# A decoder layer in fp32 on one Trainium2 core: the output projection's sums, subtractions and loads put at other places, and early heads' work stepped once per piece

## The chip, the cores and the metric

The kernel runs on one core of a Trainium2 chip. The core has five engines with a queue of instructions each: TensorE (PE in the profile, with its weight loads as PEld), VectorE (DVE), ScalarE (ACT), GpSimd (POOL) and SyncE (SP), which here issues the DMAs. An engine works its queue in order, and semaphores hold it until what it reads is there. The metric is the device time of one execution in microseconds (us), the median of several runs.

## The reference

The kernel computes one layer of a hybrid decoder on 512 tokens with 2048 features, in float32:

```python
h = rms_norm(x, norm1_w)
q, k, v, z, xbc, dt_raw = split(h @ w_in)     # 8 heads x 128; 16 SSD heads x 64
attn = moba_attention(rms_norm(q), rms_norm(k), v)          # causal, blocks of 256
ssm = grouped_rms_norm(ssd_chunked_scan(silu(conv4(xbc)), dt) * silu(z))
x = x + concat([attn, ssm]) @ w_out                         # out projection, 2048 x 2048
h = rms_norm(x, norm2_w)
u_gate, u_val = split(conv3(h @ w_up))                      # 2048 x (2 x 5632)
return x + (silu(u_gate) * u_val) @ w_down                  # 5632 x 2048
```

## The kernel before

Every float32 operand is split into a rounded high part and the rest (`hi` by ScalarE, `lo` = operand minus hi by VectorE), and a product is three matmuls: hi by hi, hi by lo, lo by hi.

**Stages.** From 0 to about 626 us runs the input projection. Its weights come in pieces (`pieces`), and between pieces TensorE does the small products of heads whose inputs are there: attention heads in pairs p = 0 to 3, two SSD groups. Each head's work is a Python generator (`g_q`, `g_head`, `g_ssm`, `g_pair`) that yields between steps; `spawn` starts it, and `advance` lets each waiting generator do one step if by the planner's clocks (`clk`) its input is ready. `advance` is called after each piece in the main loop and once in the middle of a piece (`fm_uses` at `kk == 2`, `tok_use` at half its order). A step's products write to `sm`, of which there are three PSUM buffers. A call of `advance` thus sets how many big products (`acc<-...`) stand between a projection's end and the step that needs its result.

Then come the three seven-product projections: out (626 to about 850 us), up (to 1660) and down (to 2130, three passes). A 2 x 2 block product is made from seven products instead of eight. Work is in **groups**: 8 for out (`m`, 0 to 7), 44 for up, 3 x 8 for down. A group has weight tiles of 128 x 1024 for its four quarters (`rawb` for "21" and "22", `rawa` for "11", "12" and "22b", `load`) and sums of them, the chain in `add`: s1 = 21 + 22, s2 = s1 − 11, s3 = 21 := 11 − 21, s4 = 12 − s. All are on VectorE but s3 (line 1044), which is on GpSimd. The chain's tile `s` lies in PSUM, but for group 0, where it is `acc_s` in SBUF. On the other side stand seven **kinds** (`cmb` tiles, KT1, K11, KT2, K21, KT3, K22, KT4): the activations' quarters and sums of them, split in high and low, used by all groups of a projection.

An **item** is one product of one group, 24 matmuls of 128 x 256 in the full case; a **slot** is the item's number. Items go P5, P3 of the group before, P1, P4 of the group before, P6, P2, P7. After each item `step_slot` issues, in this order: what stands in the table `events` for the slot, the low split of two items on (`split_lo(slot + 2)`), what stands in the table `after`, and the high split of three items on. So the order within VectorE's queue is the order of these calls; the tables are filled by `at(slot, fn, where=...)`.

**What the change touches in the out projection.** `acc(gi)` (line 1280) loads the two rows of x to which group m is added, tile `acc`, from `xT`. `down_after` (L1188) adds each finished product into it. When a row is done (P3 or P4), `out_row` scales it into `gx` (L1214, ScalarE), squares it into `sq`, adds that to `rbc` (L1212, VectorE), and on the second row makes the quarter sums of `gx` for the up projection (`sums`: L955 for 128 x 512, L957 and L958 for 128 x 256), and writes `gx` to `xd` in DRAM. For m = 7 the sums and the first two kinds of the up projection are made at once, without the trip through DRAM. `kinds_of` loads the other kinds' raw halves (`ld`, `lx`, `twin`) and splits them at given slots (`b_split`, L390 and L391, in `after`); `pairs_split` splits the part that comes from `gx`. KT2 and K21 of the out projection are loaded ready-made from `mk` (L1151).

Of the kernel before, what the change touches and what calls it, by code (L numbers as in the profile page):

```python
# [188 lines left out]
def body(ctx, tc, xT, wi, wz, wo, wu, wd0, wd1, wd2, pp, pf, outT, dbg={}):  # L189
# [151 lines left out]

    def spawn(g, urgent=False):
        step([g, 0.0, urgent, 0])

# [19 lines left out]

    def advance(force=False):

        for e in list(gens):
            e[3] += 1
            ready_ = clk["pe"] >= e[1]
            if force or (e[2] and (ready_ or e[3] > 1)) or \  # L370
                    (ready_ and max(clk["act"], clk["dve"]) < clk["pe"] + BEHIND):
                step(e)
# [106 lines left out]
    def g_ssm(g, sg):  # L479
# [101 lines left out]
        for i in range(2):  # L581
            spawn(g_pair(2 * g + i, ms[i]))

# [19 lines left out]
    def g_head(acc, hd):  # L603
# [26 lines left out]
        for half in range(2):  # L630
# [75 lines left out]
            if pr["n"] == 4:  # L706
                spawn(g_pair(4 + hd["i"] // 2, pr["m"]))

# [33 lines left out]
    def fm_uses(R, k0, nks, nk_tot, box, done):  # L742

        uses = []
        for nk in nks:
            def use(h, l, k0=k0, nk=nk):
                if k0 == 0:
                    box["acc"] = acc_tile()
                for kk in range(nk):
                    if kk == 2:  # L750
                        advance()
                    k = k0 + kk
                    rh, rl = R(k)
# [23 lines left out]
    def tok_use(k0, nk, cols, box, done):  # L777

        def use(h, l):
# [5 lines left out]
            for n, (kk, t) in enumerate(order):  # L785
                if n == len(order) // 2:
                    advance()
                k = k0 + kk
# [116 lines left out]
    def add_pair(p):  # L905
        pr = {}
        hds = [{"i": 2 * p + i, "pair": pr} for i in range(2)]
        q_, k_ = ([lambda acc, i=i, f=f: spawn(f(acc, hds[i])) for i in range(2)] for f in (g_q, g_head))
        for f in (q_[0], k_[0], q_[1]) if p < 3 else (k_[0], q_[0], k_[1], q_[1]):
# [27 lines left out]
    def z1_done(t, acc):  # L937
        A_.activation(sgs[1]["sz"][:, t, :], acc, AF.Silu, scale=rstd[:, t:t + 1])
        if t == 3:
            st["sz1"] = True  # L940
            spawn(g_ssm(1, sgs[1]))

# [80 lines left out]

    raw, chain, parts = {}, {}, {}
    cols = lambda gi: groups[gi]["n"] * 128
# [14 lines left out]
    def add(gi, name):  # L1040
        n = cols(gi)
        if name == "s3":
            r = raw[gi, "21"][:, :n]
            po.tensor_tensor(r, raw[gi, "11"][:, :n], r, op=OP.subtract)  # L1044
            return
# [25 lines left out]
    def split_lo(k):  # L1071
        if k >= len(items):
            return
        n = cols(items[k][0])
        h, src = parts[k]
# [4 lines left out]

    events, after = {}, {}

# [55 lines left out]
    def kinds_of(ph, base, todo, bufs, early, there=-99):  # L1138

        for k, ((t, q, n, src, slot), b) in enumerate(zip(todo, bufs)):  # L1140
            at(base + slot, b_split, ph, t, q, n, b, where=after)
            last = [j for j in range(k) if bufs[j] == b]
# [3 lines left out]

    for t, slot in ((KT2, -7), (K21, -4)):
        def whole(t=t):
# [5 lines left out]
    for t, slots in ((KT3, (1, 2)), (K22, (3, 4)), (KT4, (5, 6))):  # L1154
        todo += [(t, 4 * h, 4 - h, md[t][:, 4 * h:7 if h else 4], slots[h]) for h in range(2)]
    kinds_of("out", 0, todo, [0, 1, 2, 0, 1, 2], -2)
    for t, slot in ((KT2, 0), (K21, 1), (KT3, 2), (K22, 4), (KT4, 6)):
        at(slot, lambda t=t: pairs_split("out", t, 7, box["gx"][:, 1]), where=after)

# [5 lines left out]
    for t, slot in ((KT2, 9), (K21, 10), (KT3, 11), (K22, 13), (KT4, 15)):  # L1165
        at(base + slot, lambda t=t: pairs_split("up", t, 6, box["gx"]), where=after)
    for p in range(len(PASSES)):
# [33 lines left out]
    def out_row(g, r):  # L1201
# [5 lines left out]
        def square():  # L1207
            if m == 0 and r == 0:
                se.activation(rbc, a, AF.Square)
            else:  # L1210
                se.activation(box["sq"], a, AF.Square)
                ve.tensor_tensor(rbc, rbc, box["sq"], op=OP.add)  # L1212
# [3 lines left out]
        if m == 7:  # L1216
            if r:
                sums(ve, gx, 0)
                pairs_split("up", KT1, 6, box["gx"]), pairs_split("up", K11, 6, box["gx"])
                sums(ve, gx, 1)  # L1220
            square()
            return
        at(slot + 1, square, where=after)
        if r:
            at(slot + 1, sums, ve, gx, where=after)
            at(slot + 2, sy.dma_start, xd[:, m], gx)

# [52 lines left out]
    def acc(gi):  # L1280
        g = groups[gi]
        m, p = g["m"], g.get("p")
        if gi == D0:
            a = box["acc_s"].rearrange("p (a b) -> p a b", a=2)
        elif D0 < gi < D0 + 3:
# [154 lines left out]
```

## Time and profile before

| | |
|---|---|
| median of 3 runs (lowest, highest) | 2131.46 us (2129.65, 2133.74) |
| the profiled execution, its own time | 2131.46 us |
| its span | 2129.8 us |
| mean granted TensorE clock | 0.987 |
| TensorE busy | 2053.8 us, 96% |
| VectorE busy | 1675.9 us, 79% |
| ScalarE busy | 1014.9 us, 48% |
| GpSimd busy | 230.9 us, 11% |

The span goes from the first to the last instruction; the 1.7 us between it and the time lie around it. A busy time is that of instructions in work. An engine that stands in its queue on a semaphore isn't busy, and the profile names the instruction whose end released it. The granted clock is the share of full speed that TensorE got; 0.92 over 22 us means that 8% of them, 1.76 us, were lost. A row of the timeline gives start, length, engine, line, operation, tiles (written <- read) and shape, and in brackets the idle time before it and its releaser.

### The profile page before, as it was taken

The page shows a single profiled execution, that of the slowest core. Times are in us where ns is not written, and L with a number is a line of the kernel's source. Part 1 is how long each engine was busy: PE and PEld are TensorE (multiplying, and loading weights), DVE is VectorE, ACT ScalarE, POOL GpSimd, SP SyncE. Part 2 cuts the span into 40 slices and gives each one's busy share as a digit, 9 for nine tenths or more (in the row PEclk, how much of TensorE's full clock was granted, in tenths as well). Part 3 has the DMA queues.
Part 4 walks back from the last instruction along what each step waited for, and adds up shares of the span by engine and source line. Part 5 has one row for each costly group of instructions (what it writes and reads, how often), then busy time and mean ns, then how long its engine had stood idle before and what let it go on. Part 6 is the DMA issues. An engine that isn't in the chain of part 4 may idle for free.

```text
span 2129.8 us, 39110 instructions
## 1 busy us (share of the span) xinstructions
PE 2053.8 (96%) x15942; PEld 1961.0 (92%) x15942; DVE 1675.9 (79%) x2333; ACT 1014.9 (48%) x1428; POOL 230.9 (11%) x115
## 2 busy tenths in 40 slices
PE   9999999999998987999999999999999899999999
PEld 8888788888788987999999999999999899899999
DVE  6545555345568888999999999999999987977976
ACT  5433344343445345555555555555555643534533
POOL 0020000000001111011111111111111111111110
PEclk9999999999999999999999999999999999999999
DMA  5232233322256566354444544445446757757663
GB/s 193 74 108 86 70 122 97 98 93 85 80 203 232 186 236 216 131 188 156 161 164 164 187 152 164 163 167 184 154 160 211 236 200 260 253 204 267 221 197 124
DMA packets 126146, 353.96 MB, mean 166 GB/s; under 512 B 11728, under 2 KB 43664, under 8 KB 122256
## 3 DMA queue, kind: packets, MB, share of 16 engines
q1 hardware_dynamic: 125968, 351.48, 48.7%
q8 instruction: 125, 2.05, 0.4%
q14 instruction: 53, 0.43, 0.1%
HBM read 297.79 MB, written 53.64 MB: 165 GB/s over the span
## 4 chain that ended last, share of the span: by engine, by line
PE 82%; DVE 11%; DMA 2%; issue 2%; ACT 2%; SPq 0%; DVEq 0%; POOL 0%; ACTq 0%; POOLq 0%
PE x L1388 50%; PE acc L184 20%; PE y L1388 8%; PE sm L184 4%; DVE lo L1077 2%; DVE cmb L391 2%; DVE gx L955 1%; DMA acc<-xT 1%; DVE s L1051 1%; DVE acc L1188 1%; DVE s L1057 1%; DVE t L184 1%; ACT t L184 1%; ACT P L184 0%; DVE lo L184 0%
## 5 line engine op out<-in xcount | busy, mean ns | idle before, releaser
L1388 PE MATMUL x<-cmb,hi 128*128 128x256 f32 x6974 | 884.0, 279 | 30.8 <-DVE cmb L391 13.9
L1388 PEld LDWEIGHTS x<-cmb,hi 128*128 128x128 f32 x6974 | 837.5, 190 | 37.2 <-DVE cmb L391 17.3
L1388 PE MATMUL x<-cmb,lo 128*128 128x256 f32 x3422 | 465.9, 278 | 21.0 <-DVE lo L1077 16.0
L1388 PEld LDWEIGHTS x<-cmb,lo 128*128 128x128 f32 x3422 | 425.4, 189 | 22.8 <-DVE lo L1077 17.6
L1068 ACT ACTIVATE hi<-s 128x1024 fp32r<-128x1024 f32 (+1 forms) x225 | 225.5, 1002 | 352.8 <-DVE s L1051 215.0
L1044 POOL TENSOR_TENSOR rawb<-rawa,rawb 128x1024 f32<-128x1024 f32 (+1 forms) x76 | 192.8, 2537 | 1306.5 <-DVE s L1051 1278.6
L1077 DVE TENSOR_TENSOR lo<-s,hi 128x1024 fp32r<-128x1024 f32 (+1 forms) x225 | 267.2, 1188 | 18.9 <-issue 13.7
L1077 DVE TENSOR_TENSOR lo<-rawa,hi 128x1024 fp32r<-128x1024 f32 (+1 forms) x228 | 270.3, 1186 | 0.0
L1068 ACT ACTIVATE hi<-rawa 128x1024 fp32r<-128x1024 f32 (+1 forms) x228 | 234.3, 1031 | 42.5 <-PE x L1388 40.5
L184 DVE TENSOR_TENSOR lo<-raw,hi 128x512 fp32r<-128x512 f32 (+1 forms) x176 | 121.4, 691 | 152.3 <-ACT hi L184 150.8
L184 PE MATMUL acc<-A,hi 128*128 128x512 f32 x448 | 183.6, 410 | 0.7 <-ACT hi L184 0.7
L184 ACT ACTIVATE hi<-raw 128x512 fp32r<-128x512 f32 (+1 forms) x176 | 110.3, 627 | 147.4 <-PE acc L184 140.5
L184 PE MATMUL acc<-A,lo 128*128 128x512 f32 x448 | 177.8, 397 | 0.0
L184 PE MATMUL acc<-B,hi 128*128 128x512 f32 x448 | 177.7, 397 | 0.0
L1188 DVE TENSOR_TENSOR acc<-x,acc 128x256 f32<-128x256 f32 x174 | 73.3, 421 | 106.0 <-PE x L1388 99.8
L1388 PE MATMUL y<-cmb,hi 128*128 128x256 f32 x1184 | 148.0, 277 | 3.1 <-DVE cmb L391 3.1
L1233 ACT ACTIVATE cP<-x 128x256 f32<-128x256 f32 x132 | 50.7, 384 | 200.9 <-PE x L1388 200.9
L1388 PEld LDWEIGHTS y<-cmb,hi 128*128 128x128 f32 x1184 | 140.5, 188 | 3.7 <-DVE cmb L391 3.7
L184 PE MATMUL acc<-hi,A 128*128 128x256 f32 (+2 forms) x448 | 135.7, 303 | 0.0
L184 PE MATMUL acc<-hi,B 128*128 128x256 f32 (+2 forms) x448 | 133.9, 299 | 0.0
L184 PE MATMUL acc<-lo,A 128*128 128x256 f32 (+2 forms) x448 | 133.9, 299 | 0.0
L1068 ACT ACTIVATE hi<-rawb 128x1024 fp32r<-128x1024 f32 (+1 forms) x76 | 78.9, 1038 | 58.4 <-PE x L1388 31.8
(236 smaller groups left out, 2508.6 us busy)
## 6 DMA issues: line engine op xcount, KB each, us to landing
rawa<-wu SPq DMA_DIRECT2D x176, 512.0 KB, 3.8
raw<-wi SPq DMA_DIRECT2D x79, 512.0 KB, 3.7
rawa<-wd SPq DMA_DIRECT2D x64, 448.0 KB, 4.1
rawb<-wu SPq DMA_DIRECT2D x44, 512.0 KB, 4.7
gd<-gx SPq DMA_DIRECT2D x22, 1024.0 KB, 4.7
rawa<-wo SPq DMA_DIRECT2D x32, 512.0 KB, 4.8
rawa<-wd SPq DMA_DIRECT2D x32, 512.0 KB, 5.2
acc<-pd SPq DMA_DIRECT2D x16, 512.0 KB, 6.4
```

The source lines that it names most:

```text
L184: return fn(out, *args, **kw)
L391: vec.tensor_tensor(lo, src, hi.bitcast(F32), op=OP.subtract)
L955: E.tensor_tensor(g[:, 4:6, :], g[:, 1:4:2, :], g[:, 0:2, :], op=OP.subtract)
L1044: po.tensor_tensor(r, raw[gi, "11"][:, :n], r, op=OP.subtract)
L1051: ve.tensor_tensor(chain[gi][:, :n], raw[gi, "21"][:, :n], raw.pop((gi, "22"))[:, :n], op=OP.add)
L1057: ve.tensor_tensor(s_, raw[gi, "12"][:, :n], s_, op=OP.subtract)
L1068: se.activation(h[:, :n], src[:, :n], AF.Copy)
L1077: ve.tensor_tensor(l[:, :n], src[:, :n], h[:, :n].bitcast(F32), op=OP.subtract)
L1188: ve.tensor_tensor(a[:, row, half], src, a[:, row, half], op=op)
L1233: se.activation(g[x], X[:, 256:] if x == "P5" else X[:, :256], AF.Copy)
L1388: one = lambda a, b, q, first, last: pe.matmul(out, a[:, q * 128:(q + 1) * 128], b, start=first, stop=last, skip_group_check=True)
```

## The change

It has six parts.

1. `spawn` and `advance` get a flag `late`. In the middle of a piece only generators that were spawned late (attention pairs p > 1, SSD group 1, and `g_pair` of these) step; the early ones step only after a whole piece.
2. s3 of groups 0 and 1 goes from GpSimd to VectorE.
3. The x rows of group 0 are loaded into the tile `lx`, in `events` six slots ahead of P5 instead of into an `acc` tile in `after` two slots ahead. The raw halves that used `lx` in the out projection go to `twin`. The load of KT2 goes from slot −7 to slot −5.
4. The splits of kinds go to a table of their own, `kinds_at`, which `step_slot` runs behind the low split and ahead of `after`. This holds for all three projections.
5. `out_row` puts the sums of groups 0 to 4 at slots +4 and +5 behind P4, those of 5 and 6 at slot +0 (before: +1, where also s3 of the next group but one stands), and the addition to `rbc` at slot +2 or +6.
6. For m = 7 the low split of slot + 2 goes first, then the first sum and the kinds K11 and KT1; the other sums, the square and its addition go to `after`.

```diff
-    def advance(force=False):
+    def advance(force=False, late=False):
         for e in list(gens):
+            if late and not e[4]:
+                continue
...
                     if kk == 2:
-                        advance()
+                        advance(late=True)
...
-            po.tensor_tensor(r, raw[gi, "11"][:, :n], r, op=OP.subtract)
+            (ve if gi < 2 else po).tensor_tensor(r, raw[gi, "11"][:, :n], r, op=OP.subtract)
...
-            at(base + slot, b_split, ph, t, q, n, b, where=after)
+            at(base + slot, b_split, ph, t, q, n, b, where=kinds_at)
...
-    for t, slot in ((KT2, -7), (K21, -4)):
+    for t, slot in ((KT2, -5), (K21, -4)):
...
-    kinds_of("out", 0, todo, [0, 1, 2, 0, 1, 2], -2)
+    kinds_of("out", 0, todo, [0, 1, 3, 4, 0, 1], -2)
...
             if r:
+                split_lo(slot + 2)
                 sums(ve, gx, 0)
-                pairs_split("up", KT1, 6, box["gx"]), pairs_split("up", K11, 6, box["gx"])
-                sums(ve, gx, 1)
-            square()
+                pairs_split("up", K11, 6, box["gx"]), pairs_split("up", KT1, 6, box["gx"])
+                at(slot, square, where=after), at(slot, sums, ve, gx, 1, where=after), at(slot + 1, count, where=after)
...
+        d = 4 if m < 5 else 0
+        at(slot + (6 if r and m < 6 else 2), count, where=after)
         if r:
-            at(slot + 1, sums, ve, gx, where=after)
-            at(slot + 2, sy.dma_start, xd[:, m], gx)
+            at(slot + d, sums, ve, gx, 0, where=after), at(slot + d + bool(d), sums, ve, gx, 1, where=after)
+            at(slot + d + 2, sy.dma_start, xd[:, m], gx)
...
-            d = {0: 2, 1: 5, D0: 2, D0 + 1: 5, D0 + 2: 6}.get(gi, 6)
-            at(p5 - d, acc, gi, where=after)
+            d = {0: 6, 1: 5, D0: 2, D0 + 1: 5, D0 + 2: 6}.get(gi, 6)
+            at(p5 - d, acc, gi, where=after if gi else events)
...
         run(slot)
         if slot > -2:
             split_lo(slot + 2)
+        run(slot, kinds_at)
         run(slot, after)
```

What this does to the queues shows at three places. The first is VectorE's queue in an out group, where the sums stood between s1 (s<-rawb,rawa, behind which GpSimd's s3 becomes free to start) and the low split of the next product (lo2). Before:

```order
L1051 TENSOR_TENSOR s_6254<-rawb_6076,rawa_6078 128x1024
L1212 TENSOR_TENSOR rbc_115<-rbc_115,sq_5793 128x512
L955 TENSOR_TENSOR gx_5868<-gx_5868 128x512
L957 TENSOR_TENSOR gx_5868<-gx_5868 128x256
L958 TENSOR_TENSOR gx_5868<-gx_5868 128x256
L1188 TENSOR_TENSOR acc_5957<-y_6264,acc_5957 128x256
L1057 TENSOR_TENSOR s_5968<-rawa_6041,s_5968 128x1024
L1077 TENSOR_TENSOR lo2_6294<-s_6254,hi2_6262 128x1024
L1188 TENSOR_TENSOR acc_5957<-x_6090,acc_5957 128x256
L1077 TENSOR_TENSOR lo2_6327<-s_5968,hi2_6296 128x1024
L1188 TENSOR_TENSOR acc_6156<-x_6331,acc_6156 128x256
```

And now:

```order
L1054 TENSOR_TENSOR s_6253<-rawb_6076,rawa_6078 128x1024
L1192 TENSOR_TENSOR acc_5957<-y_6259,acc_5957 128x256
L1060 TENSOR_TENSOR s_5973<-rawa_6041,s_5973 128x1024
L1081 TENSOR_TENSOR lo2_6288<-s_6253,hi2_6257 128x1024
L1192 TENSOR_TENSOR acc_5957<-x_6089,acc_5957 128x256
L1081 TENSOR_TENSOR lo2_6321<-s_5973,hi2_6290 128x1024
L1192 TENSOR_TENSOR acc_6155<-x_6325,acc_6155 128x256
L1058 TENSOR_TENSOR s_6253<-s_6253,rawa_6185 128x1024
L1081 TENSOR_TENSOR lo2_6352<-rawa_6185,hi2_6323 128x1024
L958 TENSOR_TENSOR gx_5870<-gx_5870 128x512
L1192 TENSOR_TENSOR acc_5957<-x_6089,acc_5957 128x256
L1081 TENSOR_TENSOR lo2_6383<-rawa_6248,hi2_6355 128x1024
```

The rbc row and the three gx rows have left the place behind s1; the first gx sum now stands behind s2 (L1058) and a low split, and the other two a product later still.

The second is SP's queue at the start of the out projection: the weight tiles (wo), the rows of x (xT), the ready kinds KT2 (cmb3) and K21 (cmb4), and raw halves (ld). Before:

```order
L1037 DMA rawb_5800<-wo 128x1024
L1037 DMA rawa_5802<-wo 128x1024
L1151 DMA cmb3_5804<-mk3_124 128x1792 x2
L1037 DMA rawa_5807<-wo 128x1024
L1037 DMA rawa_5810<-wo 128x1024
L1151 DMA cmb4_5812<-mk4_125 128x1792 x2
L1037 DMA rawb_5815<-wo 128x1024
L1037 DMA rawa_5817<-wo 128x1024
L1114 DMA ld_5869<-md1_126 128x1024
L1114 DMA ld_5869<-md1_126 128x768
L1293 DMA acc_5892<-xT 128x512 x2
```

And now:

```order
L1040 DMA rawb_5800<-wo 128x1024
L1040 DMA rawa_5802<-wo 128x1024
L1040 DMA rawa_5804<-wo 128x1024
L1301 DMA lx_5791<-xT 128x512 x2
L1155 DMA cmb3_5809<-mk3_124 128x1792 x2
L1040 DMA rawa_5812<-wo 128x1024
L1155 DMA cmb4_5814<-mk4_125 128x1792 x2
L1040 DMA rawb_5817<-wo 128x1024
L1040 DMA rawa_5819<-wo 128x1024
L1118 DMA ld_5871<-md1_126 128x1024
L1118 DMA ld_5871<-md1_126 128x768
```

The load of x (lx) has moved from the end of this piece to the fourth row, and with it the third weight tile; the kinds cmb3 stand behind both instead of ahead of them.

The third is TensorE's queue in the first half of the input projection, where the step of a head that sums its squares (sm<-ones,t) follows the projection that made t (the acc that ends with A15). Before, at the step for which TensorE waits at 239.39 us in the trace:

```order
L184 MATMUL acc_2307<-B15_108,hi_2329 128x512
L184 MATMUL acc_2307<-A15_92,lo_2330 128x512
L184 MATMUL acc_2428<-A0_77,hi_2350 128x512
L184 MATMUL acc_2428<-B0_93,hi_2350 128x512
L184 MATMUL acc_2428<-A0_77,lo_2351 128x512
L184 MATMUL acc_2428<-A1_78,hi_2350 128x512
L184 MATMUL acc_2428<-B1_94,hi_2350 128x512
L184 MATMUL acc_2428<-A1_78,lo_2351 128x512
L184 MATMUL sm_2443<-ones_113,t_2420 128x1 x4
```

And now, where the acc before it (acc_2193) ends two rows above this piece:

```order
L184 MATMUL acc_2339<-B0_93,hi_2265 128x512
L184 MATMUL acc_2339<-A0_77,lo_2266 128x512
L184 MATMUL acc_2339<-A1_78,hi_2265 128x512
L184 MATMUL acc_2339<-B1_94,hi_2265 128x512
L184 MATMUL acc_2339<-A1_78,lo_2266 128x512
L184 MATMUL acc_2339<-A2_79,hi_2265 128x512
L184 MATMUL acc_2339<-B2_95,hi_2265 128x512
L184 MATMUL acc_2339<-A2_79,lo_2266 128x512
L184 MATMUL acc_2339<-A3_80,hi_2265 128x512
L184 MATMUL acc_2339<-B3_96,hi_2265 128x512
L184 MATMUL acc_2339<-A3_80,lo_2266 128x512
L184 MATMUL sm_2367<-ones_113,t_2331 128x1 x4
```

Six matmuls of the next projection stood between the end of one and the step, and now there are twelve.

More of the change, by code (lines that the diff above doesn't have):

```diff
@@ L340, in body, with spawn @@
     gens = []
-    def spawn(g, urgent=False):
-        step([g, 0.0, urgent, 0])
+    def spawn(g, urgent=False, late=False):
+        step([g, 0.0, urgent, 0, late])
     def step(e):
@@ L581, in g_ssm @@
         for i in range(2):
-            spawn(g_pair(2 * g + i, ms[i]))
+            spawn(g_pair(2 * g + i, ms[i]), late=g > 0)
     def g_q(acc, hd):
@@ L706, in g_head @@
             if pr["n"] == 4:
-                spawn(g_pair(4 + hd["i"] // 2, pr["m"]))
+                spawn(g_pair(4 + hd["i"] // 2, pr["m"]), late=True)
     def late_parts(i, half):
@@ L786, in use @@
                 if n == len(order) // 2:
-                    advance()
+                    advance(late=True)
                 k = k0 + kk
@@ L907, in add_pair @@
         hds = [{"i": 2 * p + i, "pair": pr} for i in range(2)]
-        q_, k_ = ([lambda acc, i=i, f=f: spawn(f(acc, hds[i])) for i in range(2)] for f in (g_q, g_head))
+        q_, k_ = ([lambda acc, i=i, f=f: spawn(f(acc, hds[i]), late=p > 1) for i in range(2)] for f in (g_q, g_head))
         for f in (q_[0], k_[0], q_[1]) if p < 3 else (k_[0], q_[0], k_[1], q_[1]):
@@ L940, in z1_done @@
             st["sz1"] = True
-            spawn(g_ssm(1, sgs[1]))
+            spawn(g_ssm(1, sgs[1]), late=True)
     wide(z1_done, lambda k: next_src("wide"), XR, tok=True)
@@ L1021, in body @@
             put(gi - d, x)
-    raw, chain, parts = {}, {}, {}
+    raw, chain, parts, lo_done = {}, {}, {}, set()
     cols = lambda gi: groups[gi]["n"] * 128
@@ L1071, in split_lo @@
     def split_lo(k):
-        if k >= len(items):
+        if k >= len(items) or k in lo_done:
             return
+        lo_done.add(k)
         n = cols(items[k][0])
@@ L1078, in split_lo @@
         parts[k] = (h, l)
-    events, after = {}, {}
+    events, after, kinds_at = {}, {}, {}
     def at(slot, fn, *args, where=events):
@@ L1155, in body @@
         todo += [(t, 4 * h, 4 - h, md[t][:, 4 * h:7 if h else 4], slots[h]) for h in range(2)]
-    kinds_of("out", 0, todo, [0, 1, 2, 0, 1, 2], -2)
+    kinds_of("out", 0, todo, [0, 1, 3, 4, 0, 1], -2)
     for t, slot in ((KT2, 0), (K21, 1), (KT3, 2), (K22, 4), (KT4, 6)):
-        at(slot, lambda t=t: pairs_split("out", t, 7, box["gx"][:, 1]), where=after)
+        at(slot, lambda t=t: pairs_split("out", t, 7, box["gx"][:, 1]), where=kinds_at)
     todo = []
@@ L1165, in body @@
     for t, slot in ((KT2, 9), (K21, 10), (KT3, 11), (K22, 13), (KT4, 15)):
-        at(base + slot, lambda t=t: pairs_split("up", t, 6, box["gx"]), where=after)
+        at(base + slot, lambda t=t: pairs_split("up", t, 6, box["gx"]), where=kinds_at)
     for p in range(len(PASSES)):
@@ L1207, in square, with count @@
         def square():
[L1208 to L1211, printed above, removed]
+            se.activation(rbc if m == 0 and r == 0 else box["sq"], a, AF.Square)
+        def count():
+            if m or r:
                 ve.tensor_tensor(rbc, rbc, box["sq"], op=OP.add)
@@ L1217, in out_row @@
             if r:
+                split_lo(slot + 2)
                 sums(ve, gx, 0)
-                pairs_split("up", KT1, 6, box["gx"]), pairs_split("up", K11, 6, box["gx"])
-                sums(ve, gx, 1)
-            square()
+                pairs_split("up", K11, 6, box["gx"]), pairs_split("up", KT1, 6, box["gx"])
+                at(slot, square, where=after), at(slot, sums, ve, gx, 1, where=after), at(slot + 1, count, where=after)
+            else:
+                square(), count()
             return
         at(slot + 1, square, where=after)
+        d = 4 if m < 5 else 0
+        at(slot + (6 if r and m < 6 else 2), count, where=after)
         if r:
-            at(slot + 1, sums, ve, gx, where=after)
-            at(slot + 2, sy.dma_start, xd[:, m], gx)
+            at(slot + d, sums, ve, gx, 0, where=after), at(slot + d + bool(d), sums, ve, gx, 1, where=after)
+            at(slot + d + 2, sy.dma_start, xd[:, m], gx)
     def up_after(g, x):
@@ L1282, in acc @@
         m, p = g["m"], g.get("p")
-        if gi == D0:
-            a = box["acc_s"].rearrange("p (a b) -> p a b", a=2)
+        if gi in (0, D0):
+            a = box["acc_s" if gi else "lx"].rearrange("p (a b) -> p a b" if gi else "p (r h) b -> p r (h b)", **{"a" if gi else "r": 2})
         elif D0 < gi < D0 + 3:
```

## The prediction

> **What bounds the kernel now.** I read the page first, then the windows by stage, then the waits of TensorE in each, the chain and the timelines where it waits.
>
> ```profile
> span 2129.8 us, 39110 instructions
> PE 2053.8 (96%) x15942; PEld 1961.0 (92%) x15942; DVE 1675.9 (79%) x2333; ACT 1014.9 (48%) x1428; POOL 230.9 (11%) x115
> ```
>
> TensorE is busy 96% of the span, and the change takes no product away. So it can only win what TensorE waits or works at half clock. The windows say where that is (columns: window, its length, then busy us of PE, PEld, DVE, ACT, POOL, then the granted clock of TensorE, the DMA share and GB/s).
>
> ```profile
> 54.00:375.00 321.00, 310.81 (x1871) 270.81 (x1869) 175.53 (x351) 136.10 (x262) 22.15 (x14) 0.98 0.29 91
> 626.00:645.00 19.00, 11.19 (x75) 10.53 (x75) 11.21 (x14) 8.59 (x13) 2.36 (x1) 0.83 1.01 401
> 690.00:712.00 22.00, 19.55 (x157) 19.35 (x156) 17.62 (x21) 9.23 (x11) 2.71 (x1) 0.92 0.62 208
> 760.00:783.00 23.00, 20.55 (x181) 20.35 (x180) 19.47 (x24) 9.24 (x11) 2.71 (x1) 1.00 0.61 202
> 805.00:868.00 63.00, 50.49 (x406) 48.80 (x405) 55.24 (x72) 36.06 (x50) 7.37 (x3) 0.95 0.54 181
> 860.00:1660.00 800.00, 799.80 (x7047) 799.54 (x7046) 756.92 (x942) 424.15 (x547) 103.37 (x42) 1.00 0.49 168
> ```
>
> The 800 us of the up products are full (799.80) and have nothing to give, though VectorE is busy there for 756.92 us, 95%. The losses lie in the first half of the in-projection, in the out projection (626 to 868) and at the turns into the down passes.
>
> **The six collisions (change: sums moved away).** The chain of waits shows one pattern per output group (start, length, what): the first sum gx, then the other sums, s and lo on VectorE, then 104 products. Here are the sums of the third and fourth of six groups, with a group of the up products at the end.
>
> ```profile
> 719.92 2.82 DVE gx L955
> ...
> 726.29 14.06 PE x L1388 x104
> ...
> 743.66 2.81 DVE gx L955
> ...
> 773.47 12.09 PE x L1388 x104
> ...
> 887.79 16.43 PE x L1388 x144
> 904.22 2.72 PE y L1388 x24
> ```
>
> From one gx row to the next is 743.66 − 719.92 = 23.74 us. A free group of seven products, 144 + 24 matmuls, takes 16.43 + 2.72 = 19.15 us. So this group loses 4.6 us. Why the first sum takes 2.8 us is in the timelines of GpSimd and VectorE.
>
> ```profile
> 719.46 2.71 POOL L1044 TENSOR_TENSOR rawb<-rawa,rawb 128x1024 f32<-128x1024 f32 x1 [20.75 <-DVE s L1051]
> 813.41 0.68 DVE L955 TENSOR_TENSOR gx<-gx 128x512 f32<-128x512 f32 x1
> 868.15 2.46 POOL L1044 TENSOR_TENSOR rawb<-rawa,rawb 128x1024 f32<-128x1024 f32 x1 [18.65 <-DVE s L1051]
> 868.76 1.22 DVE L1057 TENSOR_TENSOR s<-rawa,s 128x1024 f32<-128x1024 f32 x1
> ```
>
> The same sum takes 0.68 us at 813.41, where GpSimd is idle. At 719.92 it waits for GpSimd's subtraction (719.46 + 2.71 = 722.17) and ends at 722.74. But s<-rawa,s, one of whose inputs lies in PSUM, takes 1.22 us right in GpSimd's 868.15 to 870.61. In the changed order three such instructions stand behind s1: acc<-y, s<-rawa,s and lo<-s, 0.42 (as at 642.53 below) + 1.22 + 1.22, about GpSimd's 2.71. So I take the collision as gone and not as moved to the next instruction. The sums come three slots later. A group then asks of VectorE about 17.3 us of 19.1 (the row 760:783 has 19.47 of 23, in which 2.2 us are the blocked sum). That is 90%, less than the 95% at which the up products run without a wait. What it gives:
>
> ```profile
> PE x L1388 <- DVE lo L1077: 14.1, 6, 2.5
> PE x L1388 <- DVE acc L1188: 7.4, 3, 3.5
> PE x L1388 <- ACT hi L1068: 3.4, 1, 3.4
> PE x L1388 <- DVE cmb L391: 2.8, 4, 1.5
> ```
>
> These are TensorE's waits from 626 to 862 us (total, times, longest). The first row is the six collisions, 14.1 us. The spacing says a little more: 23.74 − 19.15 less 1.76 of half clock (below) is 2.8 us, and six of these are 17. **Term 1: −15 us**, nearer the row of waits; bounds −7.5 (half come back elsewhere in the group) and −17.
>
> Four of the six stalls also drew a stretch at half clock: 690:712 has a granted clock of 0.92, so 22 × 0.08 = 1.76 us are lost, and in the chain 104 products take 14.06 us at 726.29 against 12.09 at 773.47. **Term 2: 4 × 1.76 = −7 us**, bounds 0 and −7. The Trainium skill ("TensorE: Matmul & The Clock Gate", Part 1) gives the slow state to a TensorE that was idle for a whole window of about 3.4 us; by that, stalls of 2.5 us cost no clock and this term would be 0. The rows show the loss behind stalls of 2.5 us, so the measurement decides.
>
> **The start of the out projection (x sooner, s3 of two groups on VectorE).** The queue of SP, and what waits for it:
>
> ```profile
> 619.26 0.85 SPq L1151 DMA_DIRECT2D cmb<-mk  x2
> 624.70 0.81 SPq L1037 DMA_DIRECT2D rawa<-wo  x2
> 629.98 1.41 SPq L1293 DMA_DIRECT2D acc<-xT  x2
> 630.33 2.78 DVE L184 TENSOR_TENSOR gx<-gx 128x512 f32<-128x512 f32 x1 [1.03 <-ACT gx L184]
> 642.53 0.42 DVE L1188 TENSOR_TENSOR acc<-x,acc 128x256 f32<-128x256 f32 x1 [5.12 <-DMA acc<-xT]
> ```
>
> The DMA rings run full here (row 626:645: share 1.01, 401 GB/s), and VectorE, with everything behind it in its queue, stands until 642.53 for x. In the changed queue x is asked for right behind the third weight tile, and so some 5 us earlier and ahead of 1.8 MB of kinds (2 × 128 × 1792 × 4 bytes, 4.6 us at 401 GB/s). It costs something too: that weight tile waits until about 624.7 for its buffer (the row above), and the first kinds, issued at 619.26 before, now stand behind it, so the rings idle for some 3 to 5 us of 619 to 625. What was first (x) is early, what was early (kinds) is late, in a stage that the rings bound. The wait for x (3.5 us of the 7.4) and the blocked sum at 630.33 (2.78 against 0.68) go, and 3 us of late kinds come: **term 3: −4 us** with the half clock of this stretch, bounds +5 (the rings' idle time all on the path) and −9 (both waits of 3.4 and 3.5 and 2 us of clock). VectorE's own two subtractions, 2 × 1.14 us by s at 868, lie in the wait for data; the one of group 1 also waits in VectorE's queue for its weight tile, with lo, kinds and acc queued behind it, which is part of the +5.
>
> **The turn to the up products.** Two waits are addressed.
>
> ```profile
> 826.48 0.69 DVE L955 TENSOR_TENSOR gx<-gx 128x512 f32<-128x512 f32 x1 [0.79 <-ACT gx L1214]
> 831.62 1.21 DVE L1077 TENSOR_TENSOR lo<-rawa,hi 128x1024 fp32r<-128x1024 f32 x1
> 832.88 1.65 PE L1388 MATMUL x<-cmb,lo 128*128 128x256 f32 x6 [4.99 <-DVE uv L1320]
> 845.76 2.87 DVE L391 TENSOR_TENSOR cmb<-gx,cmb 128x512 fp32r<-128x512 f32 x1
> ```
>
> TensorE waits 4.99 us at 832.88. The profile names uv, but the product reads lo, which ended at 832.83 behind sums, kinds and rbc (826.48 to 831.62). Now the split stands ahead of the sum, and rbc and the other two sums behind it. It reads none of them, so it could run up to 831.62 − 826.48 = 5.1 us sooner; the subtraction s ahead of it (1.22) and the first product's own kinds take some of that back, and I count 3. The kind at 845.76 (2.87, beside GpSimd) now stands ahead of s1 and so ahead of GpSimd, 0.68: TensorE's wait of 1.5 for it goes. With a half-clock stretch of 805:868 (63 × 0.05 = 3.2 us) half gone, 3 + 1.5 + 1.5: **term 4: −6 us**, bounds 0 and −9. The wait for acc at 817 (VectorE full from 805 on) stays.
>
> **The down passes.** Only the order within a slot changes: kinds ahead of s1.
>
> ```profile
> PE x L1388 <- DVE cmb L391: 11.1, 12, 2.3
> ```
>
> From 1660 us on this is TensorE's longest row of waits, 11.1 us for kinds. A kind that stood behind a sum (1.09 us) comes that much earlier; once per pass and three passes: **term 5: −3 us**, bounds 0 and −6. s1 comes later by as much, which delays GpSimd; its product is several slots away.
>
> **The first half of the in-projection (early heads step once per piece).** The waits from 54 to 375 us:
>
> ```profile
> PE sm L184 <- ACT t L184: 6.5, 5, 2.4
> PE sm L184 <- DVE la L184: 1.5, 1, 1.5
> PE sm L184 <- DVE h L184: 1.3, 1, 1.3
> 236.37 0.39 PE L184 MATMUL acc<-B,hi 128*128 128x512 f32 x1
> 236.60 0.39 PE L184 MATMUL acc<-A,lo 128*128 128x512 f32 x1
> 239.39 1.87 PE L184 MATMUL sm<-ones,t 128*128 128x1 f32 x8 [2.40 <-ACT t L184]
> ```
>
> 9.3 us in all. At 239.39 TensorE comes to the head's step 6 matmuls behind the projection that feeds it, 6 × 0.23 (236.60 − 236.37) = 1.4 us; now 12 stand between, 2.7 us, so such a wait shrinks by up to 1.4: five waits for t give about 5, la and h up to 2. I count 6.5. The clock of the window (321 × 0.02 = 6.4 us lost) follows the stalls; I count 3.5. Steps that came at two places now come together with three small PSUM buffers for them, which makes new waits; I take 2 (a second 1.3 like the one for h, and a little). **Term 6: −6.5 − 3.5 + 2 = −8 us**, bounds +3 and −15. From 375 us on the order of TensorE's products is the same as before.
>
> **The sum**: −15 − 7 − 4 − 6 − 3 − 8 = −43 us. Against the profiled execution (2131.46 us, which is the median too; 1.7 us lie around its span) that is **2088.5 us**.
>
> **Rivals.** (a) *The stalls move.* GpSimd's 2.7 us still catch a VectorE instruction whose inputs both lie in SBUF as the sum's do, or one slot of a fuller VectorE is late: terms 1 and 2 halve, −11 instead of −22, 2099.5 us; if they vanish, 2110.5. For it: VectorE at 90% of a group leaves some 2 us. Against: the rows at 868. Chance 0.13. (b) *The first half gives nothing*: bunched steps wait as long as they save, term 6 is 0: 2096.5. Chance 0.15. (c) *The start does not do what it says*: x comes sooner but the kinds behind it bind, term 3 is +5: 2097.5. Chance 0.10. (d) *Slower*: the early steps become a chain. Between 54 and 375 us the products are broken by 48 bursts of small ones,
>
> ```profile
> 54.38 0.60 PE L184 MATMUL sm<-identf,rstd 128*128 128x128 f32 x4
> 374.56 0.60 PE L184 MATMUL sm<-identf,t 128*128 128x128 f32 x4
> ```
>
> the first and last here. If each burst came on with its input not ready, as at the 1.3 us wait for h, they would cost 48 × 1.3 = 62 us less today's 9.3, against 35 us of the other terms: 2131.5 − 35 + 53 = 2149.5. It decides from a mean wait of (35 + 9.3)/48 = 0.9 us per burst. Against it: today 7 waits for 48 bursts are in the rows above, and a later step has its input sooner ready. Chance 0.02. (e) *No clock comes back*: half-clock stretches stay as many as they are, and term 2 and the clock shares of the terms 3 (2), 4 (1.5) and 6 (3.5) are nothing: 14 us, 2102.5. Against it: clock 1.00 in 860:1660, where TensorE doesn't stall. Chance 0.05. The Trainium skill's rule above comes to this, since by it stalls of this length draw no half clock.
>
> **Numbers.** My forecast has 0.55, (a) 0.13, (b) 0.15, (c) 0.10, (e) 0.05, (d) 0.02. The favourable ends of the terms together are −17 − 7 − 9 − 9 − 6 − 15 = −63 us; the range begins at −57, 2074, since not all will come together, and ends at 2110, at (a) with nearly all its stalls kept. Outside I leave (d), two rivals together and the last of the favourable ends, under 2 in 10. A measurement of this kernel can tell about 0.2% (4.3 us) from no change. Faster by over that: 0.96; within: 0.02; slower: 0.02.
>
> **What would show it.** Right: the first sum at 0.68 us in every out group, the six waits for lo gone, groups 19.1 us apart, granted clock 1.00 from 690 to 805; x landed before 632; TensorE's waits from 54 to 375 near 5 us. Wrong: a VectorE row of 2.8 us beside GpSimd anywhere in a group; the time from 626 to 645 no shorter; more than 10 us of waits in the first half, or any change between 860 and 1660.

## The result and the profile after

| | before | changed |
|---|---|---|
| median of 4 runs (lowest, highest) | 2131.61 us (2129.65, 2133.74) | 2097.74 us (2093.58, 2100.21) |
| the profiled execution, its own time | 2131.46 us | 2097.06 us |
| its span | 2129.8 us | 2095.4 us |
| mean granted TensorE clock | 0.987 | 0.991 |

The ratio is 0.9839 with a 95% interval of 0.9820 to 0.9858: 33.9 us less. The forecast was 43 us less, and the measured time lies in its range. The page of the changed kernel, to set beside the two lines of before:

```profile
span 2095.4 us, 39105 instructions
PE 2042.1 (97%) x15942; PEld 1951.8 (93%) x15942; DVE 1656.0 (79%) x2335; ACT 1016.7 (49%) x1430; POOL 214.3 (10%) x113
```

TensorE issues 15942 matmuls in both kernels, and those of the out, up and down projections in the same order, so the start of one and the same matmul in both traces shows where the time went. First TensorE's timeline of before: the first out product, one early in the second out group, one in the last, and from the chain the first undisturbed up group.

```profile
628.88 1.76 PE L1388 MATMUL x<-cmb,hi 128*128 128x256 f32 x14
661.32 1.98 PE L1388 MATMUL x<-cmb,hi 128*128 128x256 f32 x16
800.61 1.98 PE L1388 MATMUL x<-cmb,hi 128*128 128x256 f32 x16
868.39 16.69 PE x L1388 x144
```

The same four in the changed kernel:

```profile
614.13 1.76 PE L1397 MATMUL x<-cmb,hi 128*128 128x256 f32 x14
648.16 2.10 PE L1397 MATMUL x<-cmb,hi 128*128 128x256 f32 x16 [0.69 <-ACT hi L1071]
764.92 2.05 PE L1397 MATMUL x<-cmb,hi 128*128 128x256 f32 x16
833.71 6.35 PE x L1397 x56
```

The differences of neighbouring rows, and of the spans for the last, give the stages:

| stage | forecast | measured |
|---|---|---|
| input projection and heads (term 6) | −8 | −14.75 |
| start of the out projection (term 3) | −4 | +1.6 |
| the out groups (terms 1 and 2) | −22 | −22.5 |
| turn to the up products (term 4) | −6 | +1.0 |
| up and down products (term 5) | −3 | +0.3 |
| sum | −43 | −34.4 |

The out groups came out as forecast. A row of GpSimd's timeline, the three rows of VectorE beside it, the group of the eight first sums (shortest, median and longest in ns), two rows of the chain and a window show them, all of the changed kernel:

```profile
680.20 2.41 POOL L1047 TENSOR_TENSOR rawb<-rawa,rawb 128x1024 f32<-128x1024 f32 x1 [16.83 <-DVE s L1054]
679.99 0.42 DVE L1192 TENSOR_TENSOR acc<-y,acc 128x256 f32<-128x256 f32 x1
680.33 1.22 DVE L1060 TENSOR_TENSOR s<-rawa,s 128x1024 f32<-128x1024 f32 x1
681.46 1.22 DVE L1081 TENSOR_TENSOR lo<-s,hi 128x1024 fp32r<-128x1024 f32 x1
L958 DVE TENSOR_TENSOR gx<-gx x8: 681/683/685, 668.9 to 793.9; 128x512 f32<-128x512 f32 x8
660.80 16.43 PE x L1397 x144
677.23 2.72 PE y L1397 x24
690.00:710.00 20.00, 20.00 (x179) 20.00 (x178) 17.50 (x25) 10.21 (x12) 2.41 (x1) 1.00 0.72 252
```

Every first sum takes 0.68 us, groups are 19.15 us apart, and the window 690:710 shows TensorE full at a granted clock of 1.00. VectorE is busy 17.50 of 20 us there, 88%.

### The profile page after: what moved, and what is told of

Its sections match the earlier page's. It is cut to its first block, busy times and chain, and to the rows that moved or that the text cites. A ratio compares the mean times of both kernels' runs of the same rounds, so it can differ in the third digit from the quotient of the medians.

```text
span 2095.4 us, 39105 instructions
## 1 busy us (share of the span) xinstructions
PE 2042.1 (97%) x15942; PEld 1951.8 (93%) x15942; DVE 1656.0 (79%) x2335; ACT 1016.7 (49%) x1430; POOL 214.3 (10%) x113
## 4 chain that ended last, share of the span: by engine, by line
PE 84%; DVE 9%; DMA 3%; issue 2%; ACT 2%; SPq 0%; POOL 0%; DVEq 0%; ACTq 0%; POOLq 0%
PE x L1397 52%; PE acc L184 19%; PE y L1397 8%; PE sm L184 4%; DVE cmb L394 2%; DVE lo L1081 2%; DVE lo L184 1%; DMA cmb<-mk 1%; DVE t L184 1%; DMA rawa<-wo 1%; ACT t L184 0%; DVE acc L1192 0%; DVE s L1054 0%; DMA acc<-pd 0%; ACT P L184 0%
## 5 line engine op out<-in xcount | busy, mean ns | idle before, releaser
L1397 PEld LDWEIGHTS x<-cmb,hi 128*128 128x128 f32 x6974 | 835.9, 189 | 35.5 <-issue 11.6
L1047 POOL TENSOR_TENSOR rawb<-rawa,rawb 128x1024 f32<-128x1024 f32 (+1 forms) x74 | 176.0, 2378 | 1303.1 <-DVE s L1054 1247.9
```

Source lines behind the costliest of these rows:

```text
L1047: (ve if gi < 2 else po).tensor_tensor(r, raw[gi, "11"][:, :n], r, op=OP.subtract)
L1397: one = lambda a, b, q, first, last: pe.matmul(out, a[:, q * 128:(q + 1) * 128], b, start=first, stop=last, skip_group_check=True)
```

## The experiments

Each stage below is read from the trace of the kernel's profiled execution by the four matmuls of the tables above. Medians are of four runs. Three chips were used, and a ratio is to the kernel before on the same chip: it took 2128.50 us on that of the experiments 1, 2, 4 and 7, 2132.53 on that of 5, 6, 9 and the first kernel of 8, and 2130.69 on that of 3, 10 and the other two kernels of 8. Where a diff shows one line of several of the same kind, this is said.

**1. Only the stepping** (before, with the first part of the change; the flag of `spawn` and the second call are left out of the piece shown).

```diff
-                        advance()
+                        advance(late=True)
```

> The kernel before with the first part of the change alone: early heads step only after a whole piece. Theory: in the changed kernel the first 12 out matmuls begin 14.8 us sooner, and all of it comes from this part, so this kernel gains 14 to 15 us: 2117 us, with TensorE's waits from 54 to 375 us near 3.5 us and a granted clock of 1.00 there. Rival 1: the waits only shrink by what twelve instead of six matmuls cover, 8 us as forecast: 2123.5. Rival 2: the gain is a matter of where half-clock stretches happen to fall and goes again in another build: under 5 us, 2127 or more.

Measured: 2116.89 us, 11.6 less (ratio 0.9941, 0.9918 to 0.9964). The first out product starts at 615.00, 13.9 us sooner, and TensorE's waits from 54 to 375 are 3.4 us, as in the changed kernel (3.5). So the whole first stage belongs to this part. The granted clock of that window is 0.99 and not the 1.00 that I had expected; term 6 below comes back to this. The six collisions are still there, and the windows of their six groups tell something of the clock (it is the third number from the end; GpSimd's busy time stands ahead of it). Two of the six:

```profile
724.00:747.00 23.00, 20.55 (x167) 20.36 (x166) 18.43 (x23) 9.24 (x11) 2.71 (x1) 0.93 0.60 205
747.00:770.00 23.00, 20.55 (x181) 20.36 (x181) 19.47 (x24) 9.25 (x11) 2.71 (x1) 1.00 0.61 203
```

Five of the six groups have 0.93, one 1.00, with the same stall in each.

**2. Only the sums** (before, with the sums of groups 0 to 6 at their new slots).

```diff
-            at(slot + 1, sums, ve, gx, where=after)
-            at(slot + 2, sy.dma_start, xd[:, m], gx)
+            d = 4 if m < 5 else 0
+            at(slot + d, sums, ve, gx, 0, where=after), at(slot + d + bool(d), sums, ve, gx, 1, where=after)
+            at(slot + d + 2, sy.dma_start, xd[:, m], gx)
```

> The kernel before with only the sums of out groups 0 to 6 moved (first sum four slots behind P4, the other two five, for groups 5 and 6 none). Theory: the first sum no longer meets GpSimd's subtraction, the six waits for lo and four half-clock stretches go, and nothing else changes: 22 us less, 2109.5, with groups 19.1 us apart. Rival 1 (the stalls move to the next VectorE instruction beside GpSimd): half of it, 2120. Rival 2 (in the changed kernel it was the moved additions to rbc or the subtractions on VectorE that made room): under 5 us, 2127 or more.

Measured: 2106.94 us, 21.6 less (ratio 0.9897, 0.9871 to 0.9923); the out groups alone −22.7. Its chain:

```profile
671.62 16.70 PE x L1389 x144
688.33 2.72 PE y L1389 x24
```

The moved sums do it all; neither the additions to rbc nor the two subtractions on VectorE are needed for it.

**3. The collision, or the full slot?** (before, the sums where they were, s3 of groups 2 to 7 on VectorE.)

```diff
-            po.tensor_tensor(r, raw[gi, "11"][:, :n], r, op=OP.subtract)
+            (ve if 1 < gi < U0 else po).tensor_tensor(r, raw[gi, "11"][:, :n], r, op=OP.subtract)
```

> The kernel before, with the sums where they were, but s3 of out groups 2 to 7 on VectorE, so that GpSimd has nothing there. Theory (the sum is blocked by GpSimd): the first sum takes 0.68 us, and VectorE instead does 1.1 us of s3 ahead of lo, so each of the six waits falls from 2.6 to about 1.5 us and draws half clock more seldom: 6 us from the waits and 2 to 7 from the clock, 2118 to 2124. Rival (the slot is too full whoever works in it): the waits stay at 2.4 us or more, 2130. Rival 2 (the place of the sums does not matter, only the block): the waits go altogether, 2109.

Measured: 2117.39 us, 13.3 less (ratio 0.9935, 0.9920 to 0.9950); the out groups −11.9. From the timeline and the windows:

```profile
671.30 0.68 DVE L955 TENSOR_TENSOR gx<-gx 128x512 f32<-128x512 f32 x1
690.50 1.23 DVE L1044 TENSOR_TENSOR rawb<-rawa,rawb 128x1024 f32<-128x1024 f32 x1
690.00:710.00 20.00, 18.48 (x161) 18.28 (x161) 16.95 (x23) 9.26 (x11) 0.00 (x0) 1.00 0.67 237
```

With GpSimd idle the sum takes 0.68 us in its old place. A wait of 1.2 to 1.5 us per group is left (20 − 18.48 in this window), and no half clock follows it in any of the six groups. What is left is s3 itself, which VectorE now does ahead of lo: it takes 1.15 us from its start to that of VectorE's next instruction (690.50 to 691.65). Before, the block was 2.82 − 0.68 = 2.14 of a stall of 2.45 us, and 2.45 − 2.14 + 1.15 = 1.46. So the block by GpSimd was nearly the whole stall, and the time lies a little under the 2118 to 2124 that the theory gave. Moving the sums removes the block without the price of s3 on VectorE, and the rest with it.

**4. The start** (changed kernel, KT2 loaded at slot −7 again).

```diff
-    for t, slot in ((KT2, -5), (K21, -4)):
+    for t, slot in ((KT2, -7), (K21, -4)):
```

> The changed kernel with the load of the ready kind KT2 back at slot -7, ahead of the third weight tile and of x. Theory: at the start of the out projection the DMA rings are the bound, and the rings' idle time while KT2 stands behind a weight tile that waits for its buffer is what eats the gain of the sooner x; with KT2 sooner the kinds' raw halves land some 4 to 5 us sooner and the first group ends that much sooner: 2093. Rival 1: the order of bytes is all that counts, and x later by what KT2 is sooner gives nothing: 2097.5. Rival 2: half of the rings' time is not theirs to give, since the first in VectorE's queue is bound by what it splits: 2095.5.

Measured: 2092.55 us (ratio 0.9825, 0.9803 to 0.9847, against 0.9839 of the changed kernel). The start stage takes 4.0 us less: −2.4 against before, where the changed kernel has +1.6. The changed kernel's SP queue, ScalarE, and the DMA share (last but one) in the 12 us ahead of the first out product:

```profile
609.94 0.33 SPq L1040 DMA_DIRECT2D rawa<-wo  x1
610.32 0.90 SPq L1301 DMA_DIRECT2D lx<-xT  x2
611.27 0.90 SPq L1155 DMA_DIRECT2D cmb<-mk  x2
630.57 1.06 ACT L393 ACTIVATE cmb<-ld 128x1024 fp32r<-128x1024 f32 x1 [7.11 <-DMA ld<-md]
602.00:614.00 12.00, 12.00 (x105) 12.00 (x104) 6.68 (x12) 4.55 (x8) 0.00 (x0) 1.00 0.50 166
```

The same in this kernel:

```profile
602.60 0.85 SPq L1155 DMA_DIRECT2D cmb<-mk  x2
608.28 0.91 SPq L1301 DMA_DIRECT2D lx<-xT  x2
624.54 1.06 ACT L393 ACTIVATE cmb<-ld 128x1024 fp32r<-128x1024 f32 x1 [3.55 <-DMA ld<-md]
600.00:612.00 12.00, 12.00 (x105) 12.00 (x105) 6.70 (x12) 4.51 (x8) 0.00 (x0) 1.00 0.78 296
```

In the changed kernel SP stands until 609.94 for the buffer of the third weight tile, with KT2 queued behind it, and the rings are half idle (0.50). With KT2 ahead they are at 0.78, and ScalarE's wait for a kind's raw half falls from 7.11 to 3.55 us. x comes as early in both: it was not KT2 that held it.

**5. s3 of the first two groups on GpSimd again** (changed kernel).

```diff
-            (ve if gi < 2 else po).tensor_tensor(r, raw[gi, "11"][:, :n], r, op=OP.subtract)
+            po.tensor_tensor(r, raw[gi, "11"][:, :n], r, op=OP.subtract)
```

> The changed kernel with s3 of the first two out groups on GpSimd again. Theory: the start of the out projection is bound by the DMA rings, so two collisions of 2 us each on VectorE there lie in the wait for data: within 1 us, 2098. Rival: they are on the path, since ScalarE's first split stands behind the first sum: 3 to 4 us slower, 2101.

Measured: 2094.99 us (ratio 0.9825, 0.9808 to 0.9842). The start stage takes +1.9 against +1.6: the second part of the change does nothing there, which fits the theory that what is blocked there lies in the wait for data (the first sum takes 1.77 us here, at 612.09, instead of 0.68). The median is 3 us under the 2098 that I expected, but the first out product starts at 610.65 in this execution, 3.5 us sooner than in the changed kernel's, in a stretch that this edit doesn't touch.

**6. The kinds behind s1 again** (changed kernel; one of two such lines).

```diff
-            at(base + slot, b_split, ph, t, q, n, b, where=kinds_at)
+            at(base + slot, b_split, ph, t, q, n, b, where=after)
```

> The changed kernel with the splits of kinds back behind s1 and s3, as before the change, in all three projections. Theory: the fourth part of the change gave little: at the turn to the up products it took 1.5 us of TensorE's wait for a kind and put 2.8 us of wait for rstd in its place, and from 1630 us on it took 3 of 14 us of waits for kinds. So this kernel is 1 to 2 us faster at the turn and up to 3 us slower in the down passes: 2097 to 2099, against 2097.7. Rival: the kinds ahead are what makes the turn as good as it is, and it gets 4 us or more slower, 2102.

Measured: 2098.69 us (ratio 0.9840, 0.9825 to 0.9855), no difference to the changed kernel that the times can tell. By stages 2.3 us are lost at the start (+3.9), which I had not expected, and 0.4 won at the turn (+0.6). TensorE's waits for kinds in the down passes are 13.2 us here and 11.0 in the changed kernel.

**7. rstd ahead of GpSimd's subtraction** (changed kernel, s3 of the second up group on VectorE).

```diff
-            (ve if gi < 2 else po).tensor_tensor(r, raw[gi, "11"][:, :n], r, op=OP.subtract)
+            (ve if gi < 2 or gi == U0 + 1 else po).tensor_tensor(r, raw[gi, "11"][:, :n], r, op=OP.subtract)
```

> The changed kernel with the subtraction s3 of the second up group on VectorE as well. Theory: in the changed kernel kinds go ahead of s1, so GpSimd's s3 starts later and rstd's power stands behind it in GpSimd's queue, and TensorE waits 2.8 us for rstd and runs 3.3 us at half clock behind it; with s3 on VectorE the power runs at once, and 2.8 to 4.5 us go: 2094. Rival: VectorE is full there, and 1.2 us more on it put the next kinds late by as much: at most 1.5 us gained, 2096.5.

Measured: 2094.97 us (ratio 0.9833, 0.9807 to 0.9859); the turn takes −1.7 against +1.0. In the changed kernel GpSimd and TensorE had:

```profile
810.66 2.40 POOL L1047 TENSOR_TENSOR rawb<-rawa,rawb 128x1024 f32<-128x1024 f32 x1 [21.18 <-DVE s L1054]
813.02 2.09 POOL L184 TENSOR_TENSOR rstd<-rstd,nhalf 128x4 f32<-128x4 f32 x1
815.16 1.11 PE L184 MATMUL y<-identf,rstd 128*128 128x128 f32 x4 [2.77 <-POOL rstd L184]
```

Here:

```profile
806.56 4.26 POOL L184 TENSOR_TENSOR rstd<-rstd,nhalf 128x4 f32<-128x4 f32 x1 [17.47 <-DVE rstd L184]
811.71 0.60 PE L184 MATMUL y<-identf,rstd 128*128 128x128 f32 x4
```

The power is done at 810.82, ahead of TensorE's step at 811.71, and nothing waits for it.

**8. Both repairs**, 4 and 7 together, on two chips, with the changed kernel on the second.

> The changed kernel with both repairs, KT2 loaded at slot -7 and s3 of the second up group on VectorE. The two gains were measured apart, 5.2 and 2.8 us by the medians, at different places, so they should add: 2089.7. Rival: the time that is won at the start shifts the half-clock stretches and a part of it goes again: 2092.

> The kernel with both repairs once more: 2089 to 2092, 6 to 8 us under the changed kernel of the same chip. Rival: the difference was one of chips, 2 us or less.

> The changed kernel once more, on the chip on which the kernel with both repairs runs again, so that the two can be compared: 2096 to 2099.

Measured: 2090.76 us (ratio 0.9803, 0.9787 to 0.9818) and 2091.94 (0.9823, 0.9806 to 0.9839); the changed kernel beside the second 2096.36 (0.9837, 0.9822 to 0.9852). The two repairs give 4 to 7 us; beside the changed kernel on one chip it is 4.4, less than the 6 to 8 that I expected. The second pair of intervals overlaps, so the gain is shown by the stages (4.0 and 2.7 us, above) rather than by one comparison of times. In the two executions with both repairs the start stage is again 4.2 and 4.0 us shorter than in the changed kernel, and the turn 1.4 and 2.4.

**9. The third pair of heads once per piece as well** (both repairs).

```diff
-        q_, k_ = ([lambda acc, i=i, f=f: spawn(f(acc, hds[i]), late=p > 1) for i in range(2)] for f in (g_q, g_head))
+        q_, k_ = ([lambda acc, i=i, f=f: spawn(f(acc, hds[i]), late=p > 2) for i in range(2)] for f in (g_q, g_head))
```

> The kernel with both repairs, and the third pair of heads steps once per piece as well. Theory: TensorE still waits 5.2 us for t from 375 to 614 us, four waits that arise as those of the first half did, six matmuls behind a projection; twelve matmuls shrink the two or three of them that belong to this pair by up to 1.4 us each, and a half-clock stretch may go: 3 to 5 us less, 2085.5. Rival: this pair's work then ends later than the projection's products that cover it, and what it loses at the end outweighs that: 2090 to 2095, with the first out product later.

Measured: 2089.55 us (2087.10 to 2096.01; ratio 0.9803, 0.9781 to 0.9825): no difference. My theory falls here. TensorE's waits for t from 375 to 612 us are 5.8 in three places instead of 5.3 in four, and the first out product comes at 617.04, later than in any other kernel with the new stepping (608.96 to 615.46). That late start says little, since the profiled execution is the slowest of the four (2096.01 us) and its granted clock from 375 to 608 us is 0.96; the waits decide. Those that are left in this half don't go with more products between.

**10. One addition to rbc sooner** (both repairs).

```diff
-        at(slot + (6 if r and m < 6 else 2), count, where=after)
+        at(slot + (6 if r and m < 5 else 3 if r and m == 5 else 2), count, where=after)
```

> The kernel with both repairs, and the addition of the sixth group's second squares to rbc three slots behind P4 instead of six. Theory: at the turn TensorE waits 1.4 and 3.2 us for acc because VectorE is full there with two additions to rbc, the sums of the seventh group and kinds; 0.6 us less of it there shortens these two waits by 0.6 us in all, which a time can't show but the trace does: 2.6 us in place of 3.2. Rival: the waits hang on ScalarE's splits of kinds, and nothing moves.

Measured: 2089.94 us (2088.99 to 2091.40; ratio 0.9809, 0.9795 to 0.9824), the fastest of the last four by its median; against the changed kernel on the same chip, 2096.36, it is 6.4 us less. From both repairs alone (2091.94, 2085.74 to 2094.76) the times can't tell it; the trace can. TensorE's waits for acc at the turn:

```profile
PE x L1397 <- DVE acc L1192: 3.6, 2, 3.0
```

With both repairs alone it is 4.9 us in three waits. Not the long wait got shorter, as I had expected, but the short one, 1.4 us, went. The long one (3.0) stands; what would remove it was not tried.

## Why the prediction was right, and where its terms were off

The sum came out nearer than its terms, and that is luck. Terms 3, 4 and 5 were forecast at −13 us together and measured +2.9, 15.9 us short; term 6 gave 6.75 us more than forecast and covered part of it. The measured time lies near that of rivals (b) and (c), 2096.5 and 2097.5 us, but the stages show another mixture: the first half gave more than forecast, and the start cost 1.6 us, not 5.

**Terms 1 and 2, the collisions and their clock: right in mechanism and size.** −22.5 for −22, and with the sums alone −22.7. Rival (a), that the stall moves to the next instruction, is refuted: behind s1 come acc<-y, s<-rawa,s and lo<-s, and they take their 0.42, 1.22 and 1.22 us beside GpSimd (the rows at 679.99 to 681.46 above). This agrees with the Trainium skill ("SBUF — State Buffer", section Who interferes with whom), by which a VectorE TENSOR_TENSOR with both inputs in SBUF contends with GpSimd's reads, and one with at most one input there does not: 2.82 us for the sum with both inputs in SBUF, 1.22 for the subtraction with one in PSUM. Experiment 3 shows the same block from the other side: 2.14 of the 2.45 us go when GpSimd has nothing there.

**Term 2 and the gate rule.** With the collisions the half-clock stretches went: the clock is 1.00 from 690 to 770 us, so rival (e) is refuted too. Stalls of 2.2 to 2.45 us drew a stretch in four of the six groups of the kernel before, stalls of 2.44 in five of six in experiment 1; the stalls of 1.2 to 1.5 us of experiment 3 drew none. The Trainium skill's rule ("TensorE: Matmul & The Clock Gate", Part 1), a whole idle window of 3.4 us, would have had none in any of them; the measurement decides. Nor is a short stall safe, as the next term shows.

**Term 6, the input projection: right in mechanism, too small.** The waits of the changed kernel from 54 to 375 us, and the window:

```profile
PE sm L184 <- DVE PTl L184: 1.0, 1, 1.0
PE acc L184 <- DVE u L184: 0.7, 1, 0.7
PE sm L184 <- DVE P L184: 0.7, 1, 0.7
PE sm L184 <- DVE la L184: 0.6, 1, 0.6
PE sm L184 <- DVE h L184: 0.5, 1, 0.5
54.00:375.00 321.00, 317.49 (x1935) 278.83 (x1934) 179.32 (x360) 142.79 (x273) 21.35 (x14) 1.00 0.31 96
```

All five waits for t are gone, and new ones (PTl, P, u) are 2.4 us together, near the 2 that I took. TensorE's idle time in the window falls from 10.2 to 3.5 us, 6.7 less, where I had 4.5 net; and the clock goes from 0.98 to 1.00, up to 6.4 us, where I counted 3.5. The term was mis-sized in the clock above all: I let half of the half-clock stretches stay, and in this execution none stayed. That the waits are short is not the whole reason. The longest of them, 0.98 us just ahead of 255 us, is there in all eleven profiled executions with the new stepping; in eight the clock of 240:260 is 1.00, and in three (experiment 1, experiment 10 and the second run of the changed kernel) it is 0.92 or 0.93. The changed kernel's two executions:

```profile
240.00:260.00 20.00, 19.03 (x124) 16.68 (x122) 12.94 (x32) 8.68 (x16) 2.01 (x2) 1.00 0.25 79
240.00:260.00 20.00, 19.02 (x114) 16.77 (x113) 12.07 (x29) 8.41 (x16) 2.02 (x2) 0.92 0.25 79
```

The rest of the 14.75 is within the spread of single executions: over the profiled executions of kernels with the old stepping the first out product starts at 628.88, 625.95 and 624.68, over those with the new at 613.2 in the mean of ten (608.96 to 615.46, the one of experiment 9 left out), 13.3 us sooner. The three executions with the stretch at 255 us have the three latest starts of the ten (615.00 to 615.46). Rivals (b) and (d) are refuted.

**Term 3, the start: wrong in sign.** The failing step is "3 us of late kinds" set against the sooner x, with the waits for x and for the blocked sum counted in full. x did land in time (VectorE adds to it at 622.08). But both waits lay in a stage that the rings bound, as the collision did (experiment 5), and what decided was the rings' idle time that I had named as a cost: share 0.50 instead of the 0.79 that the kernel before has in the 12 us ahead of its first out product, 0.29 × 12 = 3.5 us of their time. That the start is no shorter is also one of the prediction's own signs of being wrong. This is rival (c), with +1.6 for its +5; experiment 4 gives 4.0 us back by one number. Even so the stage comes to −2.4 and not to −4.

**Term 4, the turn: the waits went, and others took their place.** TensorE's waits in the turn (768 to 832 us of the changed kernel):

```profile
PE x L1397 <- DVE acc L1192: 4.6, 3, 3.0
PE x L1397 <- ACT cP L1241: 3.4, 2, 1.7
PE y L184 <- POOL rstd L184: 2.8, 1, 2.8
```

The 5.0 us for lo and the kind's 1.5 are gone, as forecast. The step that failed is "s1 comes later by as much, which delays GpSimd; its product is several slots away", written for the down passes and taken for granted here: I looked at the consumer of s3 and not at what is queued behind s3 on GpSimd, the power for rstd. Measured from one matmul shortly before it (846.48 and 810.35), s3 starts at −1.10 before (845.38) and at +0.31 now, 1.4 us later; and TensorE, without the kind's wait of 1.5, is there sooner. Together, 1.4 and 1.5, they make about the 2.8 us. Experiment 7 shows it. Waits for cP and acc grew by 1.4 and 0.7 us, for a reason that no run here isolates, and the clock lost more, not less:

```profile
770.00:790.00 20.00, 15.35 (x112) 14.63 (x111) 16.01 (x22) 10.79 (x15) 2.37 (x1) 0.91 0.97 337
790.00:830.00 40.00, 33.84 (x262) 33.11 (x261) 33.93 (x47) 26.14 (x37) 4.45 (x2) 0.91 0.46 150
```

60 × 0.09 = 5.4 us here against 3.2 before.

**Term 5, the down passes: the waits shrank as counted, and no time came of it.** TensorE's waits for kinds fell from 14.2 to 11.0 us (those of the x products from 11.1 to 7.9). Other waits grew by 1.9 there: for acc_s from 0.5 to 1.6, and for hi from none to 0.8. And the window 1625:1700, the first row below, has a clock of 0.93, 5.3 us lost, where the corresponding stretch of before has 0.98 over 80 us, 1.6. In experiment 4, with the same order of kinds, the down passes ran at full clock, the second row:

```profile
1625.00:1700.00 75.00, 66.53 (x520) 64.34 (x519) 70.32 (x92) 38.80 (x46) 6.55 (x3) 0.93 0.65 224
1619.00:2089.00 470.00, 448.07 (x3854) 441.77 (x3852) 385.27 (x485) 209.97 (x226) 53.56 (x24) 1.00 0.64 218
```

So the order alone doesn't set the clock. From one and the same product early in the up projection (the y product that starts at 865.39 us before and at 830.83 in the changed kernel) to the end, the profiled executions take 1264.0 us in the mean of the five with the old order of kinds (1262.8 to 1264.9) and 1264.4 in the mean of the nine with the new one (1263.2 to 1265.3). The 3 us of the forecast don't show in them. The step that failed is to take a shorter wait for kinds for shorter time; what other waits leave of it, 1.3 us, is too little to be told from this spread.

## What to carry to other kernels

When a step is moved within one engine's queue, look at every engine that it releases, and there at what is queued behind the released instruction: a subtraction that came 1.4 us later on GpSimd, with a wait gone that had covered it, cost 2.8 us of TensorE, because a small power for rstd stood behind it. A load that was asked for sooner gained nothing here, in a stage that the rings bound, and it cost 4.0 us where it set a gated load ahead of one that was free to start. A stall of a full TensorE has to be priced with the half clock that may follow it, here about 1.7 us behind nine of twelve stalls of 2.2 to 2.45; behind six stalls of 1.2 to 1.5 us none followed, but behind a wait of 0.98 us elsewhere one did in three of eleven executions.

## What the runs showed of the hardware

One and the same input projection with the same waits (5.2 to 5.3 us for t from 375 us on) ended between 608.96 and 615.46 us in ten executions. The granted clock differs between them, at 240:260 as shown above and later. First the window of the changed kernel, whose out products began at 614.13, then of the fastest, the second run of both repairs, with 608.96:

```profile
375.00:612.00 237.00, 231.52 (x1322) 198.78 (x1321) 124.17 (x261) 94.27 (x192) 10.31 (x12) 0.98 0.29 92
```

```profile
375.00:608.00 233.00, 227.49 (x1329) 195.41 (x1328) 123.91 (x260) 94.96 (x192) 10.33 (x12) 1.00 0.32 101
```

0.98 against 1.00 over 237 us is up to 4.7 us. So a stall of a given length draws a half-clock stretch in some executions and not in others. These starts differ by 6.5 us, as much as the times of one kernel do (2093.58 to 2100.21 for the changed one), so gains below that are read from the stages of the traces.
